# Three instead of two gate/up chunks start on half of the tokens, and the first one's weights are split by DMAs, in a two-layer encoder on one core

## The chip, the cores and the metric

The kernel runs on one core of a Trainium2 chip. The metric is the time of one execution on the device in microseconds (us). The core's engines run at the same time and wait for each other by semaphores: TensorE (PE in the profile, its weight loads apart as PEld), VectorE (DVE), ScalarE (ACT), GpSimd (POOL) and SyncE (SP, which here only issues DMAs).

## What is computed

Two layers of an encoder over 512 tokens of width 1024, in float32:

```python
for l in range(DEPTH):                                   # DEPTH = 2
    h = rms_norm(x, pre_mix_norm[l])
    proj = h @ w_in[l]                                   # 1024 -> 3072: q, k, v, conv u, gates b, c
    attn = dilated_mixture_attention(rotary(q), rotary(k), v)     # 8 heads of 64
    conv_y = gate_b * short_conv(gate_c * conv_u, conv_w[l])
    merged = concat([rms_norm(attn, attn_out_norm[l]), rms_norm(conv_y, conv_out_norm[l])])
    mix = merged @ w_out[l]                              # 1024 -> 1024
    x = x + rms_norm(mix, post_mix_norm[l])
    h = rms_norm(x, pre_ffn_norm[l])
    g, u = split(h @ w_gate_up[l])                       # 1024 -> 2 x 2816
    x = x + rms_norm((silu(g) * u) @ w_down[l], post_ffn_norm[l])   # 2816 -> 1024
```

## The kernel before

**Split products.** A float32 product is made of three matmuls of a rounded type: each operand is split in a high part (rounded) and a low part (what is left), and `mm3` (L188) adds high x high, low x high and high x low into the same PSUM bank. Weights come in chunks of 128 x 2048, loaded as two halves of 128 x 1024 (512 KB). `load_raw` (L111) puts a half into one of three `raw` buffers by an SP DMA; `split_half` (L169) makes `wh` (a rounding copy on ACT, L177) and `wl` (a subtraction on DVE, L178), in four buffers each; `take` (L180) does this up to two halves ahead of their use. With `keep` it does not go further ahead than the four buffers allow while the half `keep` is still to be used.

**Stages of a layer.** In projection with attention interleaved, convolution, out projection, feed forward (gate/up, then down). Tokens lie in four tiles of 128. The gate/up part has 22 chunks (128 columns of gate and 128 of up each); chunks 0 to 3 are made by plain split products and chunks 4 to 21 by `seven`, with seven half-size products in place of eight.

**The seam between out projection and feed forward.** `out_proj` (L633) makes the tokens' tiles one after the other. When a tile's two halves are there (`evac`, L658, with ACT and DVE), the norm of the mix, the residual (`residual`, L625) and the next norm (`normed`, L227) follow on ACT and DVE. Then PE must transpose the tile (`transposed`, L238: eight transposes of 128 x 128 into two PSUM banks), and ACT and DVE split the result into `hT` (L245, L246) and keep it unsplit (`raw`, L248). Tiles 0 and 1 are transposed within the out projection. Tiles 2 and 3 are not ready by then; so gate/up chunks 0 and 1 first run over the first 256 tokens only (`pair_part` with columns 0 to `HS`), 8 steps of 6 matmuls each. `turning(t)` puts the transposes of tile t behind step 6 (`TURN_GU`) of such a half chunk: tile 2 in chunk 0, tile 3 in chunk 1. Then the two chunks run over the other 256 tokens, and `gated_full` applies silu and the product. Chunks 2 and 3 run over all 512 tokens at once.

**What sets the order.** PE and SP take their instructions in the order of the code. ACT, DVE and POOL are ordered by a scheduler when the kernel is built; each of them, too, takes its rows strictly one after the other. Buffers are handed out from pools: `kl` has two (the low parts of the keys of a pair of heads, one pair after the other), `big` eleven of 8 KB per partition; the PSUM pools are `acc` (4 banks), `att` (3) and `pv` (1). POOL has six additions per layer around the attention and the convolution (L382), and no DMA.

Of the kernel before, what the change touches and what calls it, by code (L numbers as in the profile page):

```python
# [16 lines left out]
F32 = mybir.dt.float32  # L17
# [6 lines left out]
P = 128  # L24
# [53 lines left out]
def encoder(ctx: ExitStack, tc: tile.TileContext, x, xT, pos, mask, cols, rows, w, out):  # L78
# [26 lines left out]
    def bank(tag):  # L105
        return ps.tile([P, 512], F32, tag=tag, bufs={"acc": 4, "att": 3, "pv": 1}[tag], name=nm(tag))
# [62 lines left out]
    def split_half(i):  # L169

        if i >= 2 * DEPTH * NCHUNK or i in halves or SEVEN <= i // 2 % NCHUNK - 16 < MT:
            return
        for k in range(i, min(i + RAW_AHEAD, 2 * DEPTH * NCHUNK - 1) + 1):
            if k not in raws:
                load_raw(k)
        hi, lo = new_half(i)
        nc.scalar.copy(hi, raws[i])  # L177
        nc.vector.tensor_sub(lo, raws[i], hi.bitcast(F32))  # L178

    def take(n, h, keep=None):  # L180

# [13 lines left out]
    def mean_part(s, n):  # L195

        u = small(1)
        v = small(1)
        nc.vector.tensor_scalar(u, s, 1.0 / n, EPS, op0=ALU.mult, op1=ALU.add)
        nc.vector.tensor_scalar(v, u, -0.5, None, op0=ALU.mult)  # L200
        return u, v
# [22 lines left out]
    def new_hT():  # L224
        return [[big([P, 4, S], F32R) for _ in range(2)] for _ in range(2)]
# [405 lines left out]
    def out_proj(l, merged, sq_a, sq_c, inv):  # L631
        base = l * NCHUNK + 12
        gpost = load_row(l, 1)  # L633
        mix = [[None] * NT for _ in range(2)]
        ssq = [small(2) for _ in range(NT)]
        part0 = [None] * NT
        hT = raw = None
        hs = [None] * NT

        def part(t, f, which, tag, turn=None):  # L640
            acc = bank(tag)
            for k in range(4):
                if turn is not None and k == TURN // 2:
                    transposed(turn, hs[turn], hT, "acc", raw)
                kt = 4 * which + k
                hi, lo = take(base + 2 * f + which, k // 2, 2 * (base + 2 * f + (which if f == 0 else 0)) if t < NT - 1 else None)
                c = (k % 2) * 512
                st = merged[kt // 2]
                mm3(acc, st[:, kt % 2, 0, t * P:(t + 1) * P], st[:, kt % 2, 1, t * P:(t + 1) * P],
                    hi[:, c:c + 512], lo[:, c:c + 512], k == 0, k == 3)  # L650
            return acc

        a = [part(0, 0, 0, "acc"), part(1, 0, 0, "acc")]
        rs_a = row_scales(sq_a, "att")
        a += [part(t, 0, 0, "acc") for t in (2, 3)]
        rs_c = row_scales(sq_c, "att", inv)

        def evac(t, f, a, c):  # L658
            m = mix[f][t] = (row if f else tmp)([P, S])
            nc.scalar.activation(m, a, AF.Copy, scale=rs_a[:, 2 * t:2 * t + 1])  # L660
            nc.vector.scalar_tensor_tensor(m, c, rs_c[:, 2 * t:2 * t + 1], m, op0=ALU.mult, op1=ALU.add)
            j = row([P, S])
            nc.scalar.activation(j, m, AF.Square, accum_out=ssq[t][:, f:f + 1])
            nc.vector.tensor_mul(m, m, gpost[:, f * 512:f * 512 + 512])

        for t in range(NT):
            evac(t, 0, a[t], part(t, 0, 1, "att"))
            part0[t] = mean_part(ssq[t][:, 0:1], D)
        hT = new_hT()
        raw = [big([P, 4, S]) for _ in range(2)]  # L670
        gffn = load_row(l, 2)
        for t in range(NT):
            a = part(t, 1, 0, "att")
            c = part(t, 1, 1, "att", t - 2 if t >= 2 else None)
            evac(t, 1, a, c)
            r = rsqrt_mean(ssq[t][:, 1:2], D, part=part0[t])
            residual(t, mix, r)
            hs[t] = normed(t, gffn)
        return hT, hs, raw

    def feed_forward(l, hT, hs, raw):
# [38 lines left out]
        def gated_full(m, accs):  # L720
            sg = tmp([P, S])
            nc.scalar.activation(sg, accs[0], AF.Silu)
            gated(m, sg, accs[1])
# [114 lines left out]
            next(ahead)  # L838
            gated(m, gate, up)

        g0 = [bank("acc"), bank("acc")]
        g1 = [bank("acc"), bank("acc")]
        pair_part(base, g0, hT, 0, HS, turning(2), 2 * base)
        pair_part(base + 1, g1, hT, 0, HS, turning(3), 2 * base)
        making = make_sums()
        steps = [0]

# [2 lines left out]
            if steps[0] % 2 == 0:  # L850
                next(making, None)

        pair_part(base, g0, hT, HS, S, step)
        gated_full(0, g0)
        pair_part(base + 1, g1, hT, HS, S, step)
        gated_full(1, g1)
        ahead = None
        for m in range(2, SEVEN):
            n = [0]

            def step2(m=m, n=n):
                nonlocal ahead
                step()
                n[0] += 1
                if m == SEVEN - 1:
                    if ahead is None:
                        ahead = prepare(SEVEN)
                    if n[0] < 6:
                        next(ahead)

            gated_full(m, pair_full(base + m, hT, step2))
# [163 lines left out]
```

## Time and profile before

| | us |
|---|---|
| three timed runs, median (lowest, highest) | 1183.04 (1182.93, 1186.59) |
| the profiled execution | 1181.35 |
| its span, first to last instruction | 1179.6 |
| PE busy in the span | 1161.3 |
| DVE, ACT, POOL busy | 788.5, 628.4, 33.8 |
| granted TensorE clock, mean | 0.998 |

Times within the trace count from the start of the span. Layer 0's out projection and feed forward meet near 237 us, layer 1's near 821. A row of the timeline has start, duration, engine, line, operation, output and input tiles, form and count; where an engine stood idle before the row, the length of it and the releaser stand in brackets. In the view of groups, the numbers behind the count are busy time in us and the mean of one in ns.

### The profile page before, as it was taken

The page shows a single profiled execution, that of the slowest core. Times are in us where ns is not written, and L with a number is a line of the kernel's source. Part 1 is how long each engine was busy: PE and PEld are TensorE (multiplying, and loading weights), DVE is VectorE, ACT ScalarE, POOL GpSimd, SP SyncE. Part 2 cuts the span into 40 slices and gives each one's busy share as a digit, 9 for nine tenths or more (in the row PEclk, how much of TensorE's full clock was granted, in tenths as well). Part 3 has the DMA queues.
Part 4 walks back from the last instruction along what each step waited for, and adds up shares of the span by engine and source line. Part 5 has one row for each costly group of instructions (what it writes and reads, how often), then busy time and mean ns, then how long its engine had stood idle before and what let it go on. Part 6 is the DMA issues. An engine that isn't in the chain of part 4 may idle for free.

```text
span 1179.6 us, 17833 instructions
## 1 busy us (share of the span) xinstructions
PE 1161.3 (98%) x7000; PEld 1018.9 (86%) x7000; DVE 788.5 (67%) x1330; ACT 628.4 (53%) x1217; POOL 33.8 (3%) x55
## 2 busy tenths in 40 slices
PE   9999999989999999999999999999999999999997
PEld 7777778888999999888877777788899999998886
DVE  4798655786888888432557986458868888883323
ACT  7577544663565557331445775437636555582311
POOL 5000001000000000000000000100000000000000
PEclk9999999999999999999999999999999999999999
DMA  8221123123333333423132211322223333333221
GB/s 320 90 72 54 55 66 112 56 98 99 107 99 103 106 107 110 158 74 114 46 117 80 72 54 57 99 95 72 79 90 103 106 108 108 108 126 123 91 72 72
DMA packets 33205, 114.38 MB, mean 97 GB/s; under 512 B 3936, under 2 KB 3936, under 8 KB 33120
## 3 DMA queue, kind: packets, MB, share of 16 engines
q1 hardware_dynamic: 32400, 112.15, 29.1%
q8 instruction: 55, 0.90, 0.3%
q10 hardware_dynamic: 720, 1.09, 0.2%
q14 instruction: 30, 0.25, 0.1%
HBM read 111.12 MB, written 2.10 MB: 96 GB/s over the span
## 4 chain that ended last, share of the span: by engine, by line
PE 92%; DVE 4%; ACT 2%; issue 1%; DMA 0%; DVEq 0%; SPq 0%
PE acc L811 18%; PE att L811 13%; PE acc L190 13%; PE acc L192 13%; PE acc L191 13%; PE att L190 4%; PE att L192 4%; PE att L191 4%; PE pv L427 3%; PE att L420 2%; PE att L403 1%; PE att L404 1%; ACT mid L232 1%; PE pv L192 1%; PE pv L190 1%
## 5 line engine op out<-in xcount | busy, mean ns | idle before, releaser
L178 DVE TENSOR_TENSOR wl<-raw,wh 128x1024 fp32r<-128x1024 f32 x120 | 146.5, 1222 | 165.5 <-ACT wh L177 164.9
L177 ACT CAST wh<-raw 128x1024 fp32r<-128x1024 f32 x120 | 125.7, 1050 | 177.7 <-PE acc L192 67.4
L811 PE MATMUL acc<-big,wh 128*128 128x256 f32 x1152 | 212.0, 283 | 0.0
L190 PE MATMUL acc<-big,wh 128*128 128x512 f32 (+1 forms) x496 | 184.8, 372 | 0.0
L191 PE MATMUL acc<-big,wh 128*128 128x512 f32 (+1 forms) x496 | 180.1, 363 | 1.1 <-DVE big L246 1.1
L192 PE MATMUL acc<-big,wl 128*128 128x512 f32 (+1 forms) x496 | 180.1, 363 | 0.0
L811 PEld LDWEIGHTS acc<-big,wh 128*128 128x128 f32 x1152 | 179.8, 192 | 0.2
L811 PE MATMUL acc<-big,wl 128*128 128x256 f32 x576 | 163.0, 283 | 0.0
L811 PE MATMUL att<-big,wh 128*128 128x256 f32 x864 | 160.4, 283 | 0.0
L811 PEld LDWEIGHTS att<-big,wh 128*128 128x128 f32 x864 | 134.7, 192 | 0.2
L811 PE MATMUL att<-big,wl 128*128 128x256 f32 x432 | 122.3, 283 | 0.0
L762 DVE TENSOR_TENSOR wl<-t,wh 128x1024 fp32r<-128x1024 f32 x72 | 88.0, 1223 | 43.0 <-ACT wh L761 43.0
L761 ACT CAST wh<-t 128x512 fp32r<-128x512 f32 x144 | 88.7, 619 | 45.9 <-PE att L811 31.7
L811 PEld LDWEIGHTS acc<-big,wl 128*128 128x128 f32 x576 | 110.6, 192 | 0.0
L192 PEld LDWEIGHTS acc<-big,wl 128*128 128x128 f32 x496 | 93.6, 189 | 15.2
L190 PE MATMUL acc<-wh,big 128*128 128x512 f32 x272 | 106.4, 391 | 0.2 <-ACT wh L524 0.2
L191 PEld LDWEIGHTS acc<-big,wh 128*128 128x128 f32 x496 | 93.8, 189 | 14.5 <-DVE big L246 1.7
L191 PE MATMUL acc<-wl,big 128*128 128x512 f32 x272 | 106.1, 390 | 0.2 <-DVE wl L525 0.2
L192 PE MATMUL acc<-wh,big 128*128 128x512 f32 x272 | 105.9, 389 | 0.0
L190 PEld LDWEIGHTS acc<-big,wh 128*128 128x128 f32 x496 | 93.7, 189 | 13.7 <-issue 0.8
L190 PE MATMUL att<-wh,big 128*128 128x512 f32 x228 | 89.4, 392 | 0.0
L761 ACT CAST wh<-raw 128x512 fp32r<-128x512 f32 x108 | 63.4, 619 | 48.5 <-PE acc L811 31.3
(212 smaller groups left out, 1942.9 us busy)
## 6 DMA issues: line engine op xcount, KB each, us to landing
raw<-in_w SPq DMA_DIRECT2D x192, 512.0 KB, 3.7
gain<-in_rows SPq DMA_DIRECT2D x7, 512.0 KB, 5.6
big<-in_xT SPq DMA_DIRECT2D x8, 256.0 KB, 5.5
raw<-in_w SPq DMA_DIRECT2D x8, 256.0 KB, 5.5
x<-in_x SPq DMA_DIRECT2D x4, 512.0 KB, 7.0
out_dram<-x SPq DMA_DIRECT2D x4, 256.0 KB, 2.1
out_dram<-x ACTq DMA_DIRECT2D x4, 256.0 KB, 2.1
mask_sb<-in_mask SPq DMA_DIRECT2D x1, 448.0 KB, 7.7
```

The source lines that it names most:

```text
L177: nc.scalar.copy(hi, raws[i])
L178: nc.vector.tensor_sub(lo, raws[i], hi.bitcast(F32))
L190: nc.tensor.matmul(o, sh, mh, start=start, stop=False)
L191: nc.tensor.matmul(o, sh, ml, start=False, stop=False)
L192: nc.tensor.matmul(o, sl, mh, start=False, stop=stop)
L232: nc.scalar.activation(h[:, c], x_sb[t][:, c], AF.Square, accum_out=ss[:, f:f + 1])
L403: nc.tensor.matmul(sc, qk[:, hd, q0:q0 + P], qk[:, 2 + hd, :], start=True, stop=False)
L420: nc.tensor.transpose(tp[:, k * P:(k + 1) * P], sm[:, k * P:(k + 1) * P], ident)
L427: nc.tensor.matmul(o[hd * 64:hd * 64 + 64, half * 256:half * 256 + 256], V[:, k, hc:hc + 64], PT[hd][:, k, :], start=k == 0, stop=k == NT - 1)
L761: nc.scalar.copy(hi[:, c:c + 512], src[:, c:c + 512])
L762: nc.vector.tensor_sub(lo[:, :n], src[:, :n], hi[:, :n].bitcast(F32))
L811: nc.tensor.matmul(o[:, :HS], sh[:, c], mh[:, k, :], start=start and k == 0 and n == 0, stop=k == 3 and n == 2, skip_group_check=True)
```

## The change

```diff
@@ split_half
         for k in range(i, min(i + RAW_AHEAD, 2 * DEPTH * NCHUNK - 1) + 1):
-            if k not in raws:
+            if k not in raws and k not in halves:
                 load_raw(k)
@@ new, behind split_half
+    def split_by_dma(l, h):
+        src = w[l * NCHUNK + 16][:, h * 1024:h * 1024 + 1024]
+        if h:
+            pair = big([P, 2, 1024], F32R)
+            hi, lo = pair[:, 0, :], pair[:, 1, :]
+        else:
+            hi, lo = (sb.tile([P, 1024], F32R, tag="kl", bufs=2, name=nm("wk")) for _ in range(2))
+        nc.gpsimd.dma_start(hi, src)
+        nc.scalar.activation(lo, hi.bitcast(F32), AF.Copy, scale=-1.0)
+        nc.gpsimd.dma_start(lo, src, accum_op=ALU.add)
+        halves[2 * (l * NCHUNK + 16) + h] = (hi, lo)
@@ out_proj
             evac(t, 0, a[t], part(t, 0, 1, "att"))
             part0[t] = mean_part(ssq[t][:, 0:1], D)
+            if t < 2:
+                split_by_dma(l, t)
@@ feed_forward
-        g0 = [bank("acc"), bank("acc")]
-        g1 = [bank("acc"), bank("acc")]
-        pair_part(base, g0, hT, 0, HS, turning(2), 2 * base)
-        pair_part(base + 1, g1, hT, 0, HS, turning(3), 2 * base)
+        accs = [[bank("acc"), bank("acc")], [bank("acc"), bank("acc")], [bank("att"), bank("pv")]]
+        keep = 2 * base + 2
+        for m in range(3):
+            pair_part(base + m, accs[m], hT, 0, HS, turning(m + 1) if m else None, keep)
...
-        pair_part(base, g0, hT, HS, S, step)
-        gated_full(0, g0)
-        pair_part(base + 1, g1, hT, HS, S, step)
-        gated_full(1, g1)
+        for m in range(3):
+            pair_part(base + m, accs[m], hT, HS, S, step, keep if m == 0 else None)
+            gated_full(m, accs[m])
         ahead = None
-        for m in range(2, SEVEN):
+        for m in range(3, SEVEN):
```

Chunk 0 of the gate/up weights (chunk 16 of the layer) no longer goes through `raw`, `wh` and `wl`. For each of its halves, POOL issues a DMA that rounds the weights into `hi` on their way, ACT writes the negative of it to `lo`, and POOL issues a second DMA that adds the weights to `lo`. The first half lies in the two `kl` buffers, the second in a `big` one. Chunks 1 and 2 take the four `wh` and `wl` buffers that chunks 0 and 1 had. Chunk 2 joins the chunks that run in two halves of tokens, with its sums in an `att` and the `pv` bank. The transposes of tile 2 now stand in chunk 1 and those of tile 3 in chunk 2.

On PE, the transposes of tile 2 in layer 0 stand as follows before (`acc_2352` and `acc_2353` are the sums of chunk 0, `mid_2245` is the normalised tile 2):

```order
L190 MATMUL acc_2353<-big_2045,wh_2307 128x256
L191 MATMUL acc_2353<-big_2047,wh_2307 128x256
L192 MATMUL acc_2353<-big_2045,wl_2308 128x256
L241 MATMUL att_2404<-ident,mid_2245 128x128 x4
L241 MATMUL att_2412<-ident,mid_2245 128x128 x4
L190 MATMUL acc_2352<-big_2045,wh_2307 128x256
```

and as follows in the change (`acc_2347` and `acc_2348` are the sums of chunk 1, `mid_2250` is tile 2):

```order
L204 MATMUL acc_2348<-big_2054,wh_2387 128x256
L205 MATMUL acc_2348<-big_2056,wh_2387 128x256
L206 MATMUL acc_2348<-big_2054,wl_2388 128x256
L255 MATMUL att_2463<-ident,mid_2250 128x128 x4
L255 MATMUL att_2471<-ident,mid_2250 128x128 x4
L204 MATMUL acc_2347<-big_2054,wh_2387 128x256
```

They have moved from the first chunk's half to the second's, that is behind 48 more matmuls of 256 columns.

On POOL, the rows of layer 0 from the end of attention on are before:

```order
L382 TENSOR_TENSOR sqa_360<-sqa_360,tmp_1437 128x512
L382 TENSOR_TENSOR sqc_361<-sqc_361,tmp_1600 128x512
L382 TENSOR_TENSOR sqa_360<-sqa_360,tmp_1666 128x512
L382 TENSOR_TENSOR sqc_361<-sqc_361,tmp_1782 128x512
L382 TENSOR_TENSOR sqc_361<-sqc_361,tmp_1830 128x512
```

and in the change (`wk_1975` and `wk_1976` are the two parts of the first half, in `kl` buffers, `big_2003` holds both parts of the second):

```order
L189 DMA wk_1975<-in_w 128x1024
L396 TENSOR_TENSOR sqa_360<-sqa_360,tmp_1437 128x512
L396 TENSOR_TENSOR sqc_361<-sqc_361,tmp_1600 128x512
L191 DMA wk_1976<-in_w 128x1024
L396 TENSOR_TENSOR sqa_360<-sqa_360,tmp_1666 128x512
L189 DMA big_2003<-in_w 128x1024
L396 TENSOR_TENSOR sqc_361<-sqc_361,tmp_1782 128x512
L191 DMA big_2003<-in_w 128x1024
L396 TENSOR_TENSOR sqc_361<-sqc_361,tmp_1830 128x512
```

The code calls for the four DMAs within the out projection; the scheduler has put all of them ahead of the convolution's last addition.

On ACT, the last rows of layer 0's attention are before (`row` is a row of softmax, `mid` its transpose):

```order
L177 CAST wh_1687<-raw_1536 128x1024
L421 COPY mid_1522<-att_1620 128x4x128
L411 ACTIVATE row_1612,small_1615<-row_1612,small_1613 128x512
L421 COPY mid_1521<-att_1638 128x4x128
L421 COPY mid_1522<-att_1650 128x4x128
```

and in the change:

```order
L177 CAST wh_1687<-raw_1536 128x1024
L190 ACTIVATE wk_1976<-wk_1975 128x1024
L425 ACTIVATE row_1612,small_1615<-row_1612,small_1613 128x512
L435 COPY mid_1522<-att_1620 128x4x128
L435 COPY mid_1521<-att_1638 128x4x128
L435 COPY mid_1522<-att_1650 128x4x128
```

The first negation stands ahead of the last exponential, and one copy has moved behind that exponential. The second negation stands in the convolution stage, ahead of a cast of weights.

## The prediction

> **What bounds the kernel now.** I read the page first, for the share of each engine and the chain of work that ended last.
>
> ```profile
> PE 1161.3 (98%) x7000; PEld 1018.9 (86%) x7000; DVE 788.5 (67%) x1330; ACT 628.4 (53%) x1217; POOL 33.8 (3%) x55
> PE 92%; DVE 4%; ACT 2%; issue 1%; DMA 0%; DVEq 0%; SPq 0%
> ```
>
> TensorE (PE) is busy for 1161.3 of 1179.6 us and makes up 92% of the chain. So time can be won only where PE stands still or works at a worse rate, and any other engine matters only through what PE waits for. The next view is therefore the list of PE's waits over the whole span (releaser: total us, times, longest):
>
> ```profile
> PE att L241 <- DVE small L213: 5.7, 2, 2.8
> PE acc L191 <- DVE big L246: 1.1, 2, 0.5
> ```
>
> The first row is by far the largest: twice, once in each layer, PE stands 2.8 us before a transpose. The timeline of PE shows the place (start, duration, engine, line, form, count):
>
> ```profile
> 237.32 0.28 PE L192 MATMUL acc<-big,wl 128*128 128x256 f32 x1
> ...
> 241.28 0.28 PE L192 MATMUL acc<-big,wl 128*128 128x256 f32 x1
> 244.40 1.06 PE L241 MATMUL att<-ident,mid 128*128 128x128 f32 x8 [2.85 <-DVE small L213]
> 245.22 0.36 PE L190 MATMUL acc<-big,wh 128*128 128x256 f32 x1
> ...
> 251.06 1.04 PE L241 MATMUL att<-ident,mid 128*128 128x128 f32 x8
> 251.85 0.36 PE L190 MATMUL acc<-big,wh 128*128 128x256 f32 x1
> ...
> 825.69 0.28 PE L192 MATMUL acc<-big,wl 128*128 128x256 f32 x1
> 828.81 0.41 PE L241 MATMUL att<-ident,mid 128*128 128x128 f32 x2 [2.85 <-DVE small L213]
> ```
>
> Durations overlap, since matmuls are pipelined; the rate is the distance of starts. From 237.32 to 241.28 there are 33 steps of 256 columns, 0.120 us each. After the last one the next start would be due at 241.40 and comes at 244.40: **3.00 us lost**, and in layer 1 the same (825.69 + 0.12 to 828.81). PE waits there to transpose token tile 2, whose normalised rows DVE has not finished. Tile 3 at 251.06 shows no wait.
>
> **Part 1: the stall goes.** Before, the transpose of tile 2 stands behind 36 half-width matmuls (six steps of the first chunk, six matmuls each). Now it stands behind the whole first half of chunk 0 (48) and six steps of chunk 1 (36). The row at 237.32 is the stage's third matmul, so at the steady rate the first stands at 237.08 (and 237.08 + 36 × 0.120 is the 241.40 above). The transpose is now due at 237.08 + 84 × 0.120 = 247.16. What it needs:
>
> ```profile
> 242.98 1.28 DVE L234 SCALAR_TENSOR_TENSOR mid<-x,small,gain 128x1024 f32<-128x1024 f32 x1
> ...
> 249.10 1.28 DVE L234 SCALAR_TENSOR_TENSOR mid<-x,small,gain 128x1024 f32<-128x1024 f32 x1
> ```
>
> Tile 2 is ready at 242.98 + 1.28 = 244.26: 2.90 us of slack in place of a stall. Tile 3 is ready at 250.38 before, and is now due at 247.16 + 0.82 (the transposes, 244.40 to 245.22) + 48 × 0.120 = 253.74, with 3.36 us of slack. The smaller wait of the list (L191 for L246, 0.5 us a layer) stays: DVE's rows up to it stand as before. What could be late instead? ACT and DVE still have four halves to split in this stretch, those of chunks 1 and 2 in place of 0 and 1:
>
> ```profile
> 231.78 1.05 ACT L177 CAST wh<-raw 128x1024 fp32r<-128x1024 f32 x1
> ...
> 233.39 1.05 ACT L177 CAST wh<-raw 128x1024 fp32r<-128x1024 f32 x1
> ...
> 235.95 1.08 ACT L177 CAST wh<-raw 128x1024 fp32r<-128x1024 f32 x1
> ...
> 239.03 1.03 ACT L177 CAST wh<-raw 128x1024 fp32r<-128x1024 f32 x1
> ```
>
> So the chain to tile 2 is not relieved. One cast (1.03) now stands between the two squares of tile 2, and a copy and a square stand ahead of its last exponential (0.59 and 0.72, as rows of that size below). If all of that came out at the end, tile 2 would be 2.3 us late, still inside the 2.90; I take it at nothing. SP's queue of weight loads has the same rows in the same places: the first load of that stage now brings chunk 1 where it brought chunk 0.
>
> The other end is the start of the second halves, which read tile 3. Before, 1.44 us (12 matmuls) pass from the transposes' end at 251.85, and ACT and DVE fit in:
>
> ```profile
> 251.70 1.07 ACT L245 CAST big<-att 128x512 fp32r<-128x512 f32 x2 [3.08 <-PE att L241]
> ```
> ```profile
> 252.32 1.29 DVE L246 TENSOR_TENSOR big<-att,big 128x512 fp32r<-128x512 f32 x2 [1.93 <-ACT big L245]
> ```
>
> The same 12 matmuls remain behind the last transpose, and both engines were idle before these rows and still are. No stall there. Term: **−3.00 us per layer**; between −3.00 and −2.3 if a new wait of 0.7 us (one subtraction, half of the 1.29) came in at the second halves.
>
> **Part 2: narrower matmuls.** Chunk 2 used to run 48 matmuls over 512 columns and now runs 96 over 256. The wide rate:
>
> ```profile
> 269.68 0.39 PE L190 MATMUL acc<-big,wh 128*128 128x512 f32 x1
> ...
> 279.88 0.39 PE L190 MATMUL acc<-big,wh 128*128 128x512 f32 x1
> ```
>
> 45 steps in 10.20 us are 0.2267 each. The cost is 48 × (2 × 0.120 − 0.2267) = **+0.64 us per layer**, all of it on PE, which sets the end.
>
> [...]
>
> **Part 3: splitting chunk 0 by DMA.** Removed per layer are two casts on ACT, two subtractions on DVE and two SP loads; but chunk 2's take their places there, and chunk 3's follow later, so this only frees the time of two such pairs, 2 × 1.05 us of ACT and 2 × 1.22 of DVE, in a later stage where PE waits for neither. Added are two negations on ACT and four DMAs on POOL, and the order shows that the scheduler puts them far earlier than the out projection: the first load into a `kl` buffer that pair 2 of the heads has left, the first negation right behind the last scores of pair 3.
>
> ```profile
> 129.10 0.39 PE L404 MATMUL att<-kl,big 128*128 128x512 f32 x1
> ...
> 157.05 0.39 PE L404 MATMUL att<-kl,big 128*128 128x512 f32 x1
> ...
> 160.93 0.60 PE L420 MATMUL att<-ident,row 128*128 128x128 f32 x4
> 161.45 2.69 PE L427 MATMUL pv<-mid,big 128*64 128x256 f32 x16
> ```
> ```profile
> 156.79 1.05 ACT L177 CAST wh<-raw 128x1024 fp32r<-128x1024 f32 x1 [0.52 <-PE acc L191]
> 157.97 0.59 ACT L421 COPY mid<-att 128x512 f32<-128x512 f32 x1
> 158.46 0.72 ACT L411 ACTIVATE row<-row,small 128x512 f32<-128x512 f32 x1
> ...
> 183.26 1.05 ACT L177 CAST wh<-raw 128x1024 fp32r<-128x1024 f32 x1 [3.28 <-issue]
> ```
> ```profile
> 159.50 0.49 DVE L414 TENSOR_SCALAR row<-row,small 128x512 f32<-128x512 f32 x1
> ```
> ```profile
> raw<-in_w SPq DMA_DIRECT2D x192, 512.0 KB, 3.7
> ```
> ```profile
> L178 DVE TENSOR_TENSOR wl<-raw,wh 128x1024 fp32r<-128x1024 f32 x120 | 146.5, 1222 | 165.5 <-ACT wh L177 164.9
> ...
> L518 ACT ACTIVATE big<-big,col_sb 128x512 fp32r<-128x512 f32 x8 | 5.8, 725 | 2.9 <-DMA col_sb<-in_cols 1.7 <-DMA big<-in_xT 0.9
> ```
>
> The first load can go when pair 2's last scores are through (129.10 + 0.39) and must have landed when ACT reaches the negation at 157.84 (156.79 + 1.05): 28 us for a transfer that takes 3.7 from SP. A load issued by POOL, one that rounds, and one that adds are not in this trace. Their price is between 3.7 us and unknown; only beyond 28 us would it reach ACT, and the adding ones have until PE's first use at 237.08. I take them as hidden.
>
> The negation itself is not in the trace either: between 1.05 (a cast of that size) and 1.45 (twice the 725 ns of a scaled activation of half the size). It delays the last exponential from 158.46 to 158.9 or 159.3. Before, the scaled row was ready 1.53 us after that exponential's start (159.50 + 0.49 against 158.46), and PE transposes it at 160.93: with 158.9 the row is ready near 160.4, with 159.3 near 160.8. Two copies to `mid` come later, up to 161.1, before PE needs them at 161.45. So 0 to about 0.3 us per layer; I take 0. The second negation falls into ACT's gaps of the convolution stage (3.28 us idle ahead of the cast at 183.26), and POOL, busy for 3% of the span, has room for the DMAs.
>
> **The sum.** Per layer −3.00 + 0.64 = −2.36; two layers −4.72 us. The profiled execution took 1181.35 us (span 1179.6), which gives 1176.6. The median of the timed runs is 1183.04, 1.7 us above that execution; the same difference from it is **1178.3 us**, −0.40%, and this is the number that I predict.
>
> **Rivals.**
>
> *The wait moves.* The stall goes from tile 2, but part of it returns: at the second halves (0.7 us a layer), at the end of attention (0.3), or outside the span, where 1181.35 − 1179.6 = 1.75 us lie now and a queue of DMAs that was not in use before might add as much again. Against it speak the slacks of 2.90 and 3.36 us; for it, that two of the three places have under 0.5 us to spare. With 2 × 1.0 or 1.75 given back the time is near 1180.2, and with both near 1182.
>
> *The DMA is late, and ACT stands behind it (slower).* ACT takes its rows in order, so a first load that lands after 157.84 holds the last softmax row, its transpose, and PE. The point is 28 us after issue; beyond it each us costs about one us per layer, and from 28 + 2.36 = 30.4 us on the change loses. With 35 us the sum is 2 × (35 − 30.36), about +9, so near 1192. For it: nothing here shows a rounding or adding DMA. Against it: an ordinary one of this size takes 3.7.
>
> [...]
>
> *It does not do what it says.* If the DMAs did not wait for early buffers but really ran during the out projection, they would share it with the weight loads; PE's first use is at 237.08, and two transfers of 3.7 us with a negation of 1.45 between them, issued by 225, would still be in time. The time would be the forecast's.
>
> **How the numbers follow.** Forecast 0.56 (own range 1175.8 to 1179.4), the moved wait 0.28 (1179.4 to 1183), late DMAs or another loss 0.12 (above 1183), and 0.04 for the third rival, which ends at the forecast's time. A measurement of this kernel can tell about 0.3%, 3.5 us, from no change; so faster is what ends below 1179.5: the forecast and the third rival, 0.60. Within 0.3% is the moved wait and a mild loss, 0.30; slower 0.10. The range goes from 1175.8 (the sum at the profiled execution's own level, 1176.6, less most of the 1.1 us of the smaller wait) to 1183.0, the end of the moved wait.
>
> **What would show it.** Right: no wait of PE on L213 (its new line) in either layer, three blocks of 48 half-width matmuls with transposes inside the second and third, the wide matmuls of chunk 3 starting 2.4 us earlier relative to the out projection's end, and ACT's negation starting within 0.2 us of the cast's end. Wrong: a wait of PE on a POOL DMA, on the transposes of tile 3, or at the first matmul of the second half; an ACT wait for the loaded half; or a span that shrinks by 4.7 us while the time does not.

## The result and the profile after

| | before | after |
|---|---|---|
| median of the timed runs, us | 1183.04 (1182.68 to 1186.59, 6 runs) | 1176.92 (1176.57 to 1177.01, 6 runs) |
| ratio to before | 1 | 0.994 (95% interval 0.9927 to 0.9953) |
| profiled execution, us | 1181.35 | 1176.98 |
| its span, us | 1179.6 | 1175.2 |

The median fell by 6.1 us, the profiled execution by 4.4. Both are gains of more than 0.3%, but they are not the same number, and the difference of 1.7 us is the main thing that the prediction did not have. First the part that it had.

The page of the changed kernel, busy time and chain:

```profile
PE 1162.7 (99%) x7096; PEld 1025.1 (87%) x7096; DVE 784.0 (67%) x1326; ACT 630.0 (54%) x1217; POOL 41.6 (4%) x63
PE 90%; DVE 4%; ACT 2%; POOL 2%; issue 2%; DVEq 0%; POOLq 0%
```

PE has 96 instructions more (in each layer 96 narrow matmuls in place of 48 wide ones) and is busy 1.4 us longer, in a span that is 4.4 us shorter. PE's waits after the change (releaser: total us, times, longest):

```profile
PE att L418 <- ACT kl L383: 1.4, 2, 0.8
PE acc L205 <- DVE big L260: 1.1, 2, 0.5
PE att L158 <- DVE tmp L152: 1.1, 1, 1.1
```

The row of 5.7 us is gone and no new one stands in its place; the 0.5 us a layer at the stage's second matmul (L205, the first that reads the low parts of the tokens) is still there. The timeline of PE in layer 0 (start, duration, engine, line, form, count, what ended a wait):

```profile
237.27 0.39 PE L205 MATMUL acc<-big,wk 128*128 128x256 f32 x1 [0.53 <-DVE big L260]
...
247.33 1.03 PE L255 MATMUL att<-ident,mid 128*128 128x128 f32 x8
...
253.96 1.03 PE L255 MATMUL att<-ident,mid 128*128 128x128 f32 x8
...
256.26 0.28 PE L204 MATMUL acc<-big,wk 128*128 128x256 f32 x1
```

The transposes of tile 2 start at 247.33 and those of tile 3 at 253.96, without a wait, where the prediction had 247.16 and 253.74. The second halves begin at 256.26, 0.12 after the matmul before them, so there is no wait at that place either. What the transposes read was there early (DVE):

```profile
243.20 1.28 DVE L248 SCALAR_TENSOR_TENSOR mid<-x,small,gain 128x1024 f32<-128x1024 f32 x1
...
248.06 1.28 DVE L248 SCALAR_TENSOR_TENSOR mid<-x,small,gain 128x1024 f32<-128x1024 f32 x1
```

Tile 2 is ready at 244.48, 2.85 us ahead of PE; tile 3 at 249.34, 4.62 ahead. The DMA split, by ACT's timeline, POOL's, and the page's list of DMA issues (KB each, median us from issue to landing):

```profile
156.94 1.05 ACT L177 CAST wh<-raw 128x1024 fp32r<-128x1024 f32 x1 [0.52 <-PE acc L205]
157.89 1.06 ACT L190 ACTIVATE wk<-wk 128x1024 fp32r<-128x1024 f32 x1
158.85 0.71 ACT L425 ACTIVATE row<-row,small 128x512 f32<-128x512 f32 x1
```
```profile
129.97 0.78 POOL L189 DMA_DIRECT2D wk<-in_w  x1 [14.31 <-PE att L418]
...
159.26 1.20 POOL L191 DMA_DIRECT2D wk<-in_w  x1 [4.44 <-ACT wk L190]
```
```profile
wk<-in_w POOLq DMA_DIRECT2D x4, 512.0 KB, 6.0
big<-in_w POOLq DMA_DIRECT2D x4, 512.0 KB, 4.9
```

The first load is issued at 129.97, right behind the scores that free its buffer, and lands in about 6 us (the median of its group); ACT comes for it at 157.89, after 28 us. No engine waits for a DMA of POOL within the layers.

The end of the kernel is another matter. The last output DMA of before, of the change and of engine_split (a run below, without POOL's DMAs):

```profile
1176.57 0.34 ACTq L940 DMA_DIRECT2D out_dram<-x  x1
```
```profile
1171.90 0.34 ACTq L955 DMA_DIRECT2D out_dram<-x  x1
```
```profile
1172.02 0.34 ACTq L956 DMA_DIRECT2D out_dram<-x  x1
```

From there to the end of the span (1179.57, 1175.20 and 1175.02) it is 3.00, 3.30 and 3.00 us. The four kept traces without a DMA of POOL have 2.99 to 3.00, the others with them 3.30 to 3.31, but for two_held with 4.26, which is not explained. In the change, SP runs twelve instructions on semaphores in the rows of the kernel's end (L1046), and eight in before (L1031). So the DMAs cost **0.30 us** once per execution.

### The profile page after: what moved, and what is told of

Its sections match the earlier page's. It is cut to its first block, busy times and chain, and to the rows that moved or that the text cites. A ratio compares the mean times of both kernels' runs of the same rounds, so it can differ in the third digit from the quotient of the medians.

```text
span 1175.2 us, 18024 instructions
## 1 busy us (share of the span) xinstructions
PE 1162.7 (99%) x7096; PEld 1025.1 (87%) x7096; DVE 784.0 (67%) x1326; ACT 630.0 (54%) x1217; POOL 41.6 (4%) x63
## 4 chain that ended last, share of the span: by engine, by line
PE 90%; DVE 4%; ACT 2%; POOL 2%; issue 2%; DVEq 0%; POOLq 0%
PE acc L827 18%; PE att L827 13%; PE acc L204 12%; PE acc L205 12%; PE acc L206 12%; PE att L204 4%; PE att L206 4%; PE att L205 4%; PE pv L441 3%; PE att L434 2%; PE att L417 1%; PE att L418 1%; PE pv L206 1%; PE pv L205 1%; PE pv L204 1%
## 5 line engine op out<-in xcount | busy, mean ns | idle before, releaser
L178 DVE TENSOR_TENSOR wl<-raw,wh 128x1024 fp32r<-128x1024 f32 x116 | 141.6, 1221 | 165.3 <-ACT wh L177 164.7
L177 ACT CAST wh<-raw 128x1024 fp32r<-128x1024 f32 x116 | 121.7, 1051 | 176.7 <-PE acc L206 67.4
L827 PEld LDWEIGHTS acc<-big,wh 128*128 128x128 f32 x1152 | 179.8, 192 | 0.2
L204 PE MATMUL acc<-big,wh 128*128 128x512 f32 (+1 forms) x400 | 154.1, 385 | 0.0
L206 PE MATMUL acc<-big,wl 128*128 128x512 f32 (+1 forms) x400 | 149.6, 374 | 0.0
L205 PE MATMUL acc<-big,wh 128*128 128x512 f32 (+1 forms) x400 | 149.3, 373 | 0.0
L827 PEld LDWEIGHTS acc<-big,wl 128*128 128x128 f32 x576 | 110.6, 192 | 0.0
L205 PE MATMUL acc<-wl,big 128*128 128x512 f32 x272 | 106.0, 390 | 0.0
L204 PE MATMUL att<-wh,big 128*128 128x512 f32 x228 | 89.4, 392 | 0.0
L206 PE MATMUL att<-wh,big 128*128 128x512 f32 x228 | 88.8, 390 | 0.0
L205 PE MATMUL att<-wl,big 128*128 128x512 f32 x228 | 88.8, 389 | 0.0
L206 PEld LDWEIGHTS acc<-big,wl 128*128 128x128 f32 x400 | 75.3, 188 | 14.0
L204 PEld LDWEIGHTS acc<-big,wh 128*128 128x128 f32 x400 | 75.4, 189 | 12.3 <-issue 0.8
```

The source lines that it names most:

```text
L204: nc.tensor.matmul(o, sh, mh, start=start, stop=False)
L205: nc.tensor.matmul(o, sh, ml, start=False, stop=False)
L206: nc.tensor.matmul(o, sl, mh, start=False, stop=stop)
L827: nc.tensor.matmul(o[:, :HS], sh[:, c], mh[:, k, :], start=start and k == 0 and n == 0, stop=k == 3 and n == 2, skip_group_check=True)
```

## The experiments

All were timed in five rounds beside the kernel before, on the same chip within a set of four. The stage is always the seam of layer 0 (the same holds in layer 1 near 820 to 840 us).

### Which part of the change brings the gain

**turn_back.** The change, but with the transposes of tiles 2 and 3 back in chunks 0 and 1:

```diff
-            pair_part(base + m, accs[m], hT, 0, HS, turning(m + 1) if m else None, keep)
+            pair_part(base + m, accs[m], hT, 0, HS, turning(m + 2) if m < 2 else None, keep)
```

> The change, with one part undone: tile 2 is again transposed in chunk 0 and tile 3 in chunk 1; three half chunks and the DMA split stay. Theory (the place of tile 2's transposes on PE makes the gain): the wait of 2.85 us on the normalised tile 2 is back in both layers, the cost of the third half chunk stays, so 1176.9 + 6.0 = 1182.9 us. Rival (splitting chunk 0 by DMA frees ACT and DVE and so makes the gain): tile 2 is ready earlier, no such wait, 1177 to 1178 us.

Measured: 1185.12 us (1184.1 to 1186.88, 11 runs), ratio 1.0019 (1.001 to 1.0027). PE's waits have the old row again:

```profile
PE att L255 <- DVE small L227: 5.7, 2, 2.9
```

So the gain needs the transposes in their new place; three half chunks and DMAs do not bring it by themselves. But the time is 2.2 us above the 1182.9 expected; its trace leads to the clock, below.

**dma_only.** The kernel before with `split_by_dma` for chunk 0, still two half chunks:

```diff
...
+            if t < 2:
+                split_by_dma(l, t)
...
+        accs = [[bank("acc"), bank("acc")], [bank("acc"), bank("acc")]]
+        for m in range(2):
+            pair_part(base + m, accs[m], hT, 0, HS, turning(m + 2), 2 * base)
...
```

> Chunk 0 split by DMAs as in the change, but only two half chunks as before, with tile 2's transposes in chunk 0. Theory: the scheduler still puts four other casts and subtractions ahead of tile 2's norm, so the wait stays at 2.4 to 2.9 us per layer and only the cost of the third half chunk is saved: 1176.9 + 6.0 - 1.3 = 1181.6 us (1180.5 to 1182). Rival (two splits fewer ahead of tile 2): tile 2 is ready 2.4 us earlier, wait under 0.7 us, 1177 us or less.

Measured: 1184.11 us (1183.16 to 1187.07, 12 runs), ratio 1.0009 (0.9999 to 1.0019), with the 5.7 us of waits unchanged. The expected 1181.6 was missed by 2.5 us, and its runs show clocks of 0.993 to 0.997. The DMA split alone brings nothing.

**engine_split.** The change with chunk 0 split by ACT and DVE from two more SP loads in the out projection:

```diff
-        nc.gpsimd.dma_start(hi, src)
-        nc.scalar.activation(lo, hi.bitcast(F32), AF.Copy, scale=-1.0)
-        nc.gpsimd.dma_start(lo, src, accum_op=ALU.add)
...
+        load_raw(i)
+        nc.scalar.copy(hi, raws[i])
+        nc.vector.tensor_sub(lo, raws[i], hi.bitcast(F32))
...
```

> The change, but chunk 0 is split by ACT and DVE, out of two more SP loads in the first half of the out projection, into the same buffers; no DMA is issued by POOL. Theory (the DMAs keep two casts and two subtractions per layer out of a stretch where DVE is nearly full): tiles become ready later and the small waits ahead of the feed forward grow by 0.2 to 2.4 us per layer; 1178.5 us (1177.3 to 1181.8). Rival (the DMAs only fill the buffers, ACT and DVE had the time): 1176.9 us, within 0.4.

Measured: 1176.6 us (1176.29 to 1176.88, 5 runs), ratio 0.9943 (0.9931 to 0.9955). My theory missed by 1.9 us and the rival was right: the DMAs can be left out. In the change, they only fill the buffers. That this run is 0.3 us below the change fits the 0.30 us that its end is shorter.

**four_narrow.** The change with chunk 3, too, in two halves of 256 columns:

```diff
-            gated_full(m, pair_full(base + m, hT, step2))
+            pair = [bank("acc"), bank("acc")]
+            pair_part(base + m, pair, hT, 0, HS, None, 2 * (base + m))
+            pair_part(base + m, pair, hT, HS, S, step2)
+            gated_full(m, pair)
```

> The change, with chunk 3 too run in two halves of 256 tokens, one right after the other: 48 matmuls of 512 columns become 96 of 256 in each layer, nothing else moves. By the rates in the trace (0.120 and 0.2267 us): +0.64 us per layer, 1176.9 + 1.3 = 1178.2 us. [...]

Measured: 1178.17 us (1177.81 to 1178.31, 5 runs), 1.25 above the change. The rows of before had priced it at 2 x 0.64 = 1.28.

### Where the other 1.7 us come from

The trace of turn_back has the cause. Windows of PE in layer 0 (busy us and instructions, granted clock, share and rate of the DMAs):

```profile
241.00:243.00 2.00, 0.65 (x6) 1.00 0.30 104
243.00:245.00 2.00, 0.50 (x3) 0.69 0.79 260
245.00:247.00 2.00, 2.00 (x11) 0.50 0.41 160
247.00:249.00 2.00, 2.00 (x11) 0.50 0.00 0
249.00:251.00 2.00, 2.00 (x13) 0.61 0.05 12
251.00:253.00 2.00, 2.00 (x19) 1.00 0.00 0
```

The granted clock falls to 0.50 while PE still stands, at 243.74 by the trace's record of the clock (0.76 us before the transposes start), and comes back at 250.57, 6.83 us later. The timeline shows what that does to PE, and that layer 1 of the same execution was spared:

```profile
244.50 1.94 PE L255 MATMUL att<-ident,mid 128*128 128x128 f32 x8 [2.86 <-DVE small L227]
...
246.46 0.41 PE L205 MATMUL acc<-big,big 128*128 128x256 f32 x1
...
250.30 0.41 PE L205 MATMUL acc<-big,wh 128*128 128x256 f32 x1
...
253.89 1.03 PE L255 MATMUL att<-ident,mid 128*128 128x128 f32 x8
...
832.32 1.06 PE L255 MATMUL att<-ident,mid 128*128 128x128 f32 x8 [2.86 <-DVE small L227]
838.97 1.03 PE L255 MATMUL att<-ident,mid 128*128 128x128 f32 x8
```

From 246.46 to 250.30 there are 18 steps of 0.213 us instead of 0.120. From the transposes of tile 2 to those of tile 3 it takes 9.39 us in layer 0 and 6.65 in layer 1, after the same wait of 2.86: the fall costs **2.74 us**. In the execution of dma_only that was profiled the clock fell in both layers (span 1185.2); here its windows in layer 1:

```profile
830.00:833.00 3.00, 1.50 (x7) 0.59 0.77 264
833.00:836.00 3.00, 3.00 (x16) 0.50 0.04 18
836.00:840.00 4.00, 4.00 (x30) 0.83 0.00 0
```

And the one execution of the kernel before on which the prediction was built had no fall at either stall; layer 0:

```profile
243.00:245.00 2.00, 0.60 (x6) 1.00 0.87 299
245.00:247.00 2.00, 2.00 (x20) 1.00 0.30 121
247.00:249.00 2.00, 2.00 (x19) 1.00 0.04 8
```

(Its mean of 0.998 comes from a fall at 1175.12, behind PE's last matmul. All 14 traces have such a fall at their end; in those without another one the mean is 0.9981 to 0.9993.)

Was it typical? Each timed run lists its mean granted clock. By clock, all runs of before in these three sets, and the twelve runs of the change (six from the result, six of change_again); the count of runs, and their lowest to highest time in us:

| kernel | 0.993 to 0.995 | 0.996 | 0.997 | 0.998 | 0.999 |
|---|---|---|---|---|---|
| before (66) | 7: 1185.65 to 1186.9 | 22: 1183.93 to 1184.94 | 31: 1182.5 to 1183.65 | 6: 1181.11 to 1181.62 | none |
| change (12) | none | none | none | 5: 1176.91 to 1177.46 | 7: 1176.57 to 1177.01 |

Only 6 of 66 runs of before are like the profiled one (1181.35). By its clock, the median is a run in which the clock had fallen somewhere, and 1.7 us is what that costs at the median. The change has no such run.

Two lengths of a fall account for the levels. One of 3.41 us, in layer 0 of two_held, cost 1.50 us (18 steps from 251.59 to 255.25 in place of 18 x 0.120); one of 6.83 us cost 2.74. As an estimate, 1181.35 with a short fall is 1182.85, with a long one 1184.09, with both 1185.59, and with two long ones 1186.83. The runs of before lie at 1182.5 to 1183.65, 1183.93 to 1184.94, 1185.65 to 1186.02 and 1186.67 to 1186.9. So the median run had, by this estimate, one short fall.

That the stall is what brings the clock down was tested by filling it.

**before_filled.** The kernel before, with 22 matmuls of 256 columns ahead of tile 2's transposes, whose results nobody uses:

```diff
                 if n[0] == TURN_GU:
+                    if t == 2:
+                        y = bank("pv")
+                        for _ in range(22):
+                            nc.tensor.matmul(y[:, :HS], hT[0][0][:, 0, :P], hT[0][0][:, 0, :HS], start=True, stop=True)
                     transposed(t, hs[t], hT, "att", raw)
```

> The kernel before, with 22 matmuls of 256 columns (22 x 0.120 = 2.64 us, results unused) put on TensorE right ahead of the transposes of tile 2, so that the stall of 2.85 us a layer is filled with work and no useful work moves. If the clock falls after the stall in part of the executions, and that is the term missing from the forecast: the time becomes that of the kernel before without a fall, about 1181.3 (its fastest runs 1181.1 to 1181.5), with a spread under 0.7 us, and the granted clock stays at 1.00 between 243 and 251 us. Rival, the spread has another cause: the median stays near 1183.5, with runs from 1181 to 1186.

Measured: 1181.55 us (1181.35 to 1182.99, 12 runs), against 1183.23 for before in the same set; ratio 0.9984 (0.9975 to 0.9992). Eleven of the 12 runs lie between 1181.35 and 1181.67, one at 1182.99; the clock is 0.998 to 0.999 in all. The transposes start 0.07 us later than before (244.40):

```profile
241.47 2.80 PE L734 MATMUL pv<-big 128*128 128x256 f32 x22
244.47 1.06 PE L241 MATMUL att<-ident,mid 128*128 128x128 f32 x8 [0.21 <-DVE small L213]
```

Useless work in the stall makes the kernel 1.7 us faster, and no useful work was moved, so the missing term is the clock. The one run at 1182.99 has a mean clock of 0.999 like the others; its cause is open.

**two_turn7 and two_turn8.** How short must the idle time be? dma_only, with the transposes of tile 2 one and two steps later:

```diff
-                if n[0] == TURN_GU:
+                if n[0] == (7 if t == 2 else TURN_GU):
```
```diff
-                if n[0] == TURN_GU:
+                if n[0] == (8 if t == 2 else TURN_GU):
```

> The DMA split with two half chunks as before, and the transposes of tile 2 one step (6 matmuls, 0.72 us) later. The stall should be 3.00 - 0.72 = 2.28 us a layer. Without any fall of the clock the time is 1181.3 - 2 x 0.72 = 1179.9. If the clock falls only after stalls of nearly 3 us: 1179.9 +-0.5 with a spread under 1 us. If 2.3 us of idle are enough for it: a median of 1181.5 or more with a spread of several us.

> The DMA split with two half chunks as before, and the transposes of tile 2 two steps (12 matmuls, 1.44 us) later: a stall of about 1.56 us a layer. Without a fall of the clock the time is 1181.3 - 2 x 1.44 = 1178.4. If an idle of 1.5 us is too short to bring the clock down: a spread under 1 us around 1178.4, clock 0.998 to 0.999 in all runs. If it still does in part of the executions: a median above 1179.2 and runs 1.5 us and more apart.

Measured for two_turn7: 1182.03 us (1180.34 to 1183.67, 12 runs), ratio 0.9986 (0.9976 to 0.9996). Its waits are of 2.1 us:

```profile
PE att L255 <- DVE small L227: 4.3, 2, 2.1
```

The two runs at a clock of 0.999 took 1180.34 and 1180.49, the three at 0.995 took 1183.3 to 1183.67: as an estimate from these means and times, the clock fell in part of the executions after an idle of 2.1 us, too. The traced one had no fall.

Measured for two_turn8: 1180.76 us (1180.6 to 1181.13, 8 runs), ratio 0.9977 (0.9967 to 0.9986), with 0.999 in all eight. Its timeline:

```profile
244.59 1.06 PE L255 MATMUL att<-ident,mid 128*128 128x128 f32 x8 [1.43 <-DVE small L227]
...
250.72 1.06 PE L255 MATMUL att<-ident,mid 128*128 128x128 f32 x8 [0.77 <-DVE mid L248]
```

The clock did not fall after 1.43 us: it is 1.00 in each window of this trace from 239 to 255 us. The expected 1178.4 was missed by 2.4 us, of which a new wait gives 2 x 0.77: with less ahead of them, tile 3's transposes come due before its norm is done. Of the other 0.8, 0.30 is the longer end; the rest I did not trace.

**The same wait, with a fall in one layer and none in the other.** All waits at tiles 2 and 3 of more than 1 us, and what the traces' record of the clock has there (times in us):

| run, layer | PE stands | length | clock |
|---|---|---|---|
| turn_back, 0 | 241.65 to 244.50 | 2.86 | falls at 243.74, 2.09 into the wait, for 6.83 |
| turn_back, 1 | 829.46 to 832.32 | 2.86 | stays |
| dma_only, 0 | 241.56 to 244.41 | 2.85 | falls at 243.44, 1.88 into the wait, for 6.83 |
| dma_only, 1 | 828.65 to 831.50 | 2.85 | falls at 830.54, 1.89 into the wait, for 6.83 |
| two_held, 0 | 247.72 to 250.33 | 2.61 | falls at 251.63, 1.30 behind the wait, for 3.41 |
| two_held, 1 | 833.00 to 835.61 | 2.61 | falls at 835.31, 2.31 into the wait, for 3.41 |
| before, 0 | 241.56 to 244.40 | 2.85 | stays |
| before, 1 | 825.97 to 828.81 | 2.85 | stays |
| two_turn7, 0 | 242.51 to 244.64 | 2.13 | stays |
| two_turn7, 1 | 826.38 to 828.52 | 2.14 | stays |
| two_turn8, 0 | 243.16 to 244.59 | 1.43 | stays |
| two_turn8, 1 | 827.19 to 828.60 | 1.42 | stays |

In five of the eight waits of 2.61 to 2.86 us, or just behind them, the clock fell, in three it did not; in turn_back the same 2.86 us went both ways within one execution. None of the four waits of 1.42 to 2.14 us in these traces has a fall. The falls came 1.88 to 2.31 us into a wait, and once 1.30 behind its end. Their lengths of 3.41 and 6.83 us are one and two times 3.413, and two falls in one trace are whole multiples of that apart, too: 587.10 us between the two falls of dma_only (172 times) and 583.68 between those of two_held (171 times). What decides whether a wait of one length brings the clock down was not shown.

### Can the same be had for less?

**held_back.** The change, with the cast and subtraction of chunk 1's halves queued behind the split of tile 1:

```diff
+        if i in behind:
+            act, dve = behind[i]
+            with tc.issue_after(act):
+                nc.scalar.copy(hi, raws[i])
+            with tc.issue_after(dve):
+                nc.vector.tensor_sub(lo, raws[i], hi.bitcast(F32))
+            return
...
+        behind[2 * base + 2] = behind[2 * base + 3] = turned[1]
```

> The change, with the cast and the subtraction of chunk 1's two halves queued behind the split of tile 1's transposes. The theory is that the wait of 0.5 us a layer at the first middle matmul (L205 for DVE's L260, kept by the change) ends because DVE subtracts those halves first: without them it goes, and the time is 1176.9 - 2 x 0.5 = 1175.9 (+-0.4), as long as the halves are ready for chunk 1's first matmul, 5.8 us later. Rival: the wait is the length of the transposes' own copy and subtraction, and stays: 1176.9 +-0.4. A worse end: chunk 1's halves come late, and PE waits at chunk 1's first matmul: above 1177.5.

Measured: 1176.08 us (1175.65 to 1176.45, 5 runs), ratio 0.9934 (0.9922 to 0.9946). The wait at the stage's second matmul is gone:

```profile
236.64 0.28 PE L211 MATMUL acc<-big,wk 128*128 128x256 f32 x1
236.96 0.39 PE L212 MATMUL acc<-big,wk 128*128 128x256 f32 x1
```

It stands 0.32 us behind the first matmul, where in the change it followed after 0.81. That is 0.49 in layer 0, as expected; the median fell by 0.84, where 1.0 was expected with 0.4 either way.

**two_held.** The same holding back with two half chunks, so without the third one's 0.64 us a layer:

```diff
...
-        for m in range(3):
-            pair_part(base + m, accs[m], hT, 0, HS, turning(m + 1) if m else None, keep)
+        for m in range(2):
+            pair_part(base + m, accs[m], hT, 0, HS, turning(m + 2), 2 * base)
...
```

> Two half chunks in place of three, the DMA split kept, and the same holding back of chunk 1's halves. If what made tile 2 late was the order in which ACT and DVE took the halves' casts and subtractions (not the number of half-width matmuls ahead of the transposes), tile 2 is ready near 239 us, ahead of its due time of about 240.7, no stall is left, and the third half-width chunk is saved (2 x 0.64): 1175.9 - 1.3 = 1174.6 (+-0.5). Rival, tile 2's norm is bound by its own chain: the stall of 2.8 us returns in both layers, 1180 or more.

Measured: 1182.42 us (1180.84 to 1184.22, 12 runs), ratio 0.9987 (0.9977 to 0.9996). A miss, and half of the theory stands. Tile 2 is in time, but now tile 3 is late (PE, then DVE):

```profile
240.94 1.04 PE L265 MATMUL att<-ident,mid 128*128 128x128 f32 x8
...
250.33 0.85 PE L265 MATMUL att<-ident,mid 128*128 128x128 f32 x6 [2.61 <-DVE mid L255]
```
```profile
240.77 1.22 DVE L182 TENSOR_TENSOR wl<-raw,wh 128x1024 fp32r<-128x1024 f32 x1
...
242.03 1.22 DVE L182 TENSOR_TENSOR wl<-raw,wh 128x1024 fp32r<-128x1024 f32 x1
...
243.83 0.74 DVE L652 SCALAR_TENSOR_TENSOR x<-tmp,small,x 128x512 f32<-128x512 f32 x1
...
245.81 1.22 DVE L185 TENSOR_TENSOR wl<-raw,wh 128x1024 fp32r<-128x1024 f32 x1
...
247.01 1.22 DVE L185 TENSOR_TENSOR wl<-raw,wh 128x1024 fp32r<-128x1024 f32 x1
...
248.90 1.28 DVE L255 SCALAR_TENSOR_TENSOR mid<-x,small,gain 128x1024 f32<-128x1024 f32 x1
```

The two subtractions that left tile 2's way stand in tile 3's, whose residual starts at 243.83, and the next two (L185) stand between that residual and tile 3's norm at 248.90. Tile 3 is ready at 250.18, hardly earlier than before (250.38), but without the stall at tile 2 PE stands ready for it from 247.72 on, where its transposes came at 251.06 before.

**two_order and engine_two.** Two half chunks with an order by hand; in engine_two chunk 0 is also split by ACT and DVE, as in engine_split:

```diff
-        behind[2 * base + 2] = behind[2 * base + 3] = turned[1]
+        behind[2 * base + 2] = turned[1][0], anchor['norm', 2]
+        behind[2 * base + 3] = anchor['xexp'], anchor['x', 3]
+        behind[2 * base + 4] = behind[2 * base + 5] = anchor['normexp'], anchor['norm', 3]
...
+            if t == 2 and raw is not None:
+                with tc.issue_after(anchor['norm', 3]):
+                    nc.vector.tensor_sub(lo, b4, hi.bitcast(F32))
...
```

> Two half chunks and the DMA split, with ACT's and DVE's work on the halves queued by hand: chunk 1's first half behind the norm of tile 2, its second half behind the residual of tile 3, chunk 2's halves and tile 2's own split behind the norm of tile 3. The run with the halves only held behind tile 1's split had no stall at tile 2 (240.94 us) but one of 2.6 us at tile 3, whose residual stood behind two subtractions (240.77 to 243.16). By the rows of that run tile 3 is now ready near 247.1 to 247.3, when its transposes are due (247.26): no stall over 0.3 us, and 2 x 0.64 us less of half-width matmuls than with three: 1174.6 (+-0.6), spread under 1 us. So the order of two engines would do what the third half chunk does, for less. Rival, tile 3's chain cannot be that short: a stall of 1 us or more at tile 3 in each layer, above 1176.5.

> The same with chunk 0 split by ACT and DVE from two more SP loads during the out projection, without the DMAs of POOL. If the DMAs only fill buffers early and ACT and DVE have the time (as the run of the change without them showed): within 0.4 us of the run with DMAs, 1174.6. Rival: with the longer order ACT and DVE no longer have it, tile 2 or 3 comes late: 1176 or more.

Measured: 1176.01 us (1175.91 to 1176.61, 5 runs) and 1175.99 (1175.64 to 1176.58, 5 runs); ratios 0.9936 (0.9924 to 0.9948) and 0.9935 (0.9924 to 0.9947). For two_order that lies between theory and rival; for engine_two it is at the rival's bound (1176), but equal to the run with the DMAs, as the theory had it. In two_order, PE and ACT at tile 3:

```profile
248.18 0.60 PE L268 MATMUL att<-ident,mid 128*128 128x128 f32 x4
249.25 0.66 PE L268 MATMUL att<-ident,mid 128*128 128x128 f32 x4 [0.47 <-ACT big L279]
```
```profile
246.12 1.98 ACT L180 CAST wh<-raw 128x1024 fp32r<-128x1024 f32 x2
248.61 0.59 ACT L279 COPY big<-att 128x512 f32<-128x512 f32 x1 [0.52 <-DVE big L275]
```

The first four transposes of tile 3 come without a wait, so tile 3 is in time. The second four wait for a PSUM bank that ACT's copy of tile 2 still reads; ACT does that copy behind DVE's subtraction of tile 2 (L275), which I had held behind the norm of tile 3. My own edit gives back about 0.65 us a layer (1.07 from 248.18 to 249.25, where four transposes take 0.41), which is all of the 0.64 that the third chunk's matmuls had cost.

**change_again.** The change once more, beside these:

> The change once more, beside the others on the same chip: 1176.9 (+-0.4), spread under 1 us, clock 0.998 to 0.999.

Measured: 1176.96 us (1176.67 to 1177.46, 6 runs), ratio 0.9942 (0.993 to 0.9954). So held_back, two_order and engine_two, all three at about 1176.0, are 0.9 us below the change (held_back was timed in another set than change_again), and engine_two needs neither the third half chunk nor a DMA of POOL.

## Why the prediction came out as it did

**The stall goes (part 1): right.** No wait is left at tile 2 or 3; the slack of tile 2 was 2.85 us (2.90 worked out). From the transposes of tile 1 (start at 234.00 before, 234.17 after) to the second group of transposes of the next layer (585.93, 583.69), the time fell from 351.93 to 349.52 us, that is by 2.41 a layer; in layer 1, from those of tile 1 (818.41, 816.16) to the start of the last matmul (1172.61, 1167.95), from 354.20 to 351.79, 2.41 again. The sum of parts 1 and 2 was 2.36. Tile 3's slack was larger than I had it (4.62 for 3.36). I had left its norm at 249.10, where it stood before; it came at 248.06, since ACT and DVE no longer split tile 2 in the middle of tile 3's chain (ACT's split of tile 2 starts at 247.97, at 245.07 before).

**Narrower matmuls (part 2): right.** four_narrow bought one more such chunk for 1.25 us, with 1.28 worked out.

**The DMA split (part 3): no cost in the layers, as predicted, 0.30 us at the kernel's end, and no gain.** The negation took 1.06 us, the lower end of my bounds, and the last exponential started at 158.85 where I had 158.9. In layer 1, where the same rows stand, the time from the first transposes of its input (579.60 before, 577.36 after) to those of its out projection (811.72, 809.48) is 232.12 us in both. The term of 0 us missed the longer end of the span, which is there in the traces with DMAs of POOL alone. engine_split shows more than I had claimed: the split by DMA isn't needed at all.

**The sum at the profiled execution's level: right.** It gave 1176.63, and the profiled execution of the change took 1176.98. Of the 0.35 between them, about 0.30 is the longer end and 0.16 passed ahead of the first tile's transposes (227.32 before, 227.48 after); against that, parts 1 and 2 gained 0.10 more than worked out.

**The step to the median: wrong.** The step is "The median of the timed runs is 1183.04, 1.7 us above that execution; the same difference from it is 1178.3". I took the 1.7 us for an offset that both kernels share. The range, down to 1175.8, still held the result, but that was not by this mechanism. The 1.7 us was the clock, whose mean is below the profiled execution's in 60 of 66 runs of before, and it goes with the stall: the change's median lies 0.1 us below its profiled execution. So the forecast of 1178.3 is 1.4 us too high, and the missing term is named and measured by before_filled (1.7 us). One row could have warned me: the profiled 1181.35 lay below all three timed runs shown.

**The rivals.** *The wait moves* did not occur: nothing came back at the second halves, the end of attention, or outside the span (1.75 us there before, 1.8 after). Only its thought of queues that were not in use before came true, with 0.30 us inside the span, at its end. It was a real danger, though: in two_held, two_order and two_turn8 the wait did move, each time to tile 3. *The DMA is late* had 28 us of slack for a transfer that took 6. *It does not do what it says* did not occur either: the last of the four DMAs was issued at 182.02, still ahead of the convolution's last addition at 194.39, so none ran in the out projection.

**Open.** Four runs of turn_back have a clock of 0.998 and took 1184.45 to 1185.12, though its parts add up to 1182.93 without a fall (1181.35, 2 x 0.64 and 0.30). A fall of 3.41 us takes 0.0014 from the mean (half of 3.41 in 1184 us), and the fall at the end alone leaves it anywhere between 0.9981 and 0.9993, so a mean of 0.998 can hide one. With its 1.50 us the sum, an estimate, is 1184.4. No trace of such a run shows it, and up to 0.7 us stay open even so.

## What to carry to other kernels

A stall of the busiest engine can cost more than its length (here a fall of the clock added 1.50 or 2.74 us to some stalls of 2.6 to 2.9): look in the trace at the clock in it and behind it, and compare the profiled execution's time with all timed runs before carrying a difference from one to the other. When a tile is late, move its consumer behind work that is there anyway, and price that work by the distance of starts in the same kernel; then check the next tile, since the delay can move one tile on (here to tile 3: 2.61 us in two_held, 0.77 in two_turn8). Try the cheap order of two engines before a new data path: here the DMAs of POOL were not needed.

## What the hardware showed unexpectedly

In or just behind idle times of 2.6 to 2.9 us on PE the granted clock fell to 0.50 in five of eight cases in the traces, and stayed there for 3.41 or 6.83 us. After 2.1 us it fell too in part of the executions, as an estimate from the mean clocks of two_turn7's runs (0.995 in three of 12), though the one traced had no fall. At 0.50, matmuls of 256 columns stood 0.213 us apart instead of 0.120 (turn_back), and one fall cost 1.50 us in two_held and 2.74 in turn_back. After 1.43 us it did not fall in any of eight runs of two_turn8, by their means of 0.999. Changes of the clock within one trace lay whole multiples of 3.413 us apart (3.41 and 6.83 us from a fall to its end, 587.10 us between the falls of dma_only, 583.68 between those of two_held). The same wait of 2.86 us brought the clock down in layer 0 of turn_back and not in layer 1, and why was not shown.

DMAs issued by POOL for 512 KB, which round or add, landed after 4.9 and 6.0 us (medians of two groups), where SP's weight loads of that size took 3.7 before; the row of each on POOL is 0.6 to 1.2 us long. With eight of them in the kernel, its end took 0.30 us longer.
